# Mixer steps of a hybrid encoder block laid anew, and two of their products moved to GpSimd

## The chip, the cores and the metric

The kernel runs on one core of a Trainium2 chip. The metric is the device time of one launch in microseconds. Times of an unchanged kernel come as the median of several runs. The profile is that of one further execution. Engines are named as in the profile: PE is TensorE, DVE is VectorE, ACT is ScalarE, POOL is GpSimd, SP is SyncE.

## The reference

One block of a streaming encoder for 256 frames of width 2048, in float32. The input is normed, and one projection gives the columns of two mixers, which run side by side: a Mamba-2 mixer (four groups of eight heads) and an RWKV-7 mixer (32 heads of width 64). Their outputs go through one output projection, and a gated feed-forward layer of width 5632 and a last norm follow. The part that the change touches is the RWKV mixer:

```python
    kk = (k * k_k.astype(f32)).reshape(b, s, H, N)
    kk = kk / jnp.maximum(jnp.sqrt(jnp.sum(kk * kk, axis=-1, keepdims=True)), 1e-12)
    k = k * (1.0 + (a - 1.0) * k_a.astype(f32))
...
        sa = jnp.einsum('bhvk,bhk->bhv', S, a_t)
        S = S * w_t[:, :, None, :] + sa[..., None] * b_t[:, :, None, :] + v_t[..., None] * k_t[:, :, None, :]
        return S, jnp.einsum('bhvk,bhk->bhv', S, r_t)
```

The reference steps frame by frame. The result of each head is normed over its 64 columns, and to it is added a bonus, the sum of r k r_k over the head times the values v; then it is gated.

## The kernel before

Every big product is made as three passes of TensorE in a reduced float format: high part by high part, low by high and high by low. For that each weight tile, after its load (issued by SP in order), is cast on ACT to its high part whi (L192), and DVE subtracts it to get the low part wlo (L193). The raw tile, whi and wlo have four buffers each, so the two engines can be at most four tiles ahead of PE. `gemm_a` (L267) makes 96 matmuls of 128x256 in a call, 24 for each weight tile; `gemm_b` (L284) makes matmuls 512 wide, 12 for each tile.

The RWKV heads go in eight pairs of head groups, four heads to a pair, and the pair loop (L908) makes for each pair the projections k, v and r with `gemm_a`, and from pair 4 on, behind v, a quarter of an output projection with `gemm_b`. The small mixer work is cut into steps, closures that `rwkv_pair` (L444) makes: `keys2` (L520, with the key scale product kt at L526), `sums` (L548: products on DVE, the head sums `ps_sum` on PE, and the norms nn and bon), `amat` (L590, the score matrices atb and atk), `inv_out` (L628), `inv_level` and `inv_in` (L693), which send a small triangular matrix to memory and back and invert it there in blocks until X stands (L701), `lev16a` to `lev32b` (products `ps_b`), then for each of four chunks of 64 frames `step_r`, `step_w` and `step_s` (L755 to L823, matmuls `ps_r`, `ps_w`, `ps_s`, `ps_y`), and `gnorm`, `gnorm2` (the bonus product at L847) and `final`.

Where a step is issued is set by a queue: class `Side` (L42) holds steps with a due time in ticks, and the big product calls `side.tick` as it goes, four ticks for each call of `gemm_a`, so one tick is 24 matmuls. The tables PREP, AMATS, INV and CHAIN (L34 to L39) hold the due times. `window(pi, ticks)` (L882) fills the queue at the head of each pass of the loop: window pi runs the preparation of pair pi, the scores and inverse of pair pi-1 and the chain of pair pi-2. Windows 0 to 3 have 12 ticks, 4 to 7 have 16, window 8 has 20 and window 9 has 18. In windows of 12 ticks, the times of INV and CHAIN are scaled by 11.5/16. What is left at the end of a window is issued by `drain`. The framework then sets the final order on each engine by when operands are ready by its own costs.

Of the kernel before, what the change touches and what calls it, by code (L numbers as in the profile page):

```python
# [68 lines left out]
def tile_hybrid_block(ctx: ExitStack, tc: tile.TileContext, x, norm1_g, w_in, conv_w, conv_b, dt_bias, A_log, D_skip,  # L69
# [374 lines left out]
    def rwkv_pair(pi, st):  # L444
# [75 lines left out]
        def keys2():  # L520
            q, kp, ta, pin = (st[n] for n in ("q", "kp", "ta", "pin"))
            nc.vector.scalar_tensor_tensor(ta, ta, 1.0, q, ALU.add, ALU.mult)
            bt = tl("bt")
# [2 lines left out]
            nc.vector.tensor_tensor(kt, kp, pin, ALU.mult)  # L526
# [261 lines left out]
        def step_s(c):  # L788
# [34 lines left out]
            return f  # L823

        def gnorm():
            Y = st["Y"]
# [5 lines left out]
            for c in range(NCH):  # L832
                nc.scalar.activation(sq[:, c], Y[:, c], AF.Square, bias=nm[:, c:c + 1], accum_out=rs[:, c:c + 1])
            nc.scalar.activation(rs, rs, AF.Sqrt, bias=epsg, scale=1.0 / 64)
            nc.vector.reciprocal(rs, rs)
            nc.vector.tensor_tensor(nm, nm, rs, ALU.mult)
            for c in range(NCH):
                nc.scalar.activation(Y[:, c], Y[:, c], AF.Identity, bias=nm[:, c:c + 1], scale=rs[:, c:c + 1])

        def gnorm2():  # L840
            Y = st["Y"]
# [5 lines left out]
            nc.vector.tensor_tensor(vb, st["vt"], bc(st["bon"], 64), ALU.mult)  # L847
# [351 lines left out]
```

## Time and profile before

| what | value |
|---|---|
| median of three runs | 1671.96 us (1670.29, 1671.96, 1674.27) |
| the profiled execution's own time | 1671.13 us |
| its span, first to last instruction | 1669.4 us |
| mean granted TensorE clock | 0.996 |
| weights and inputs read from memory | 281.75 MB |

In the trace, window 0 begins at 38.1 us, window 1 at 76.6, window 2 at 117.8, window 3 at 185.9, window 4 at 242.2, window 5 at 309.0, window 6 at 376.5, window 7 at 443.7, window 8 at 510.6 and window 9 at 585.8 and ends at 652.9. The rest of the span is the Mamba mixer, the output projection and the feed-forward layer. A row of the table of windows has the stretch, its length, the busy time of each engine with its number of instructions, the granted clock and the DMA engines' share. A row of the timeline has the start, the duration, engine, line, operation, tiles out and in, and, in brackets, how long the engine stood idle and who released it.

### The profile page before, as it was taken

The numbers are of one execution on the slowest core, as the hardware profiler recorded it, in microseconds if no ns is written. First come the engines' busy times: TensorE is split into PE (matmuls) and PEld (weight loads), VectorE is DVE, ScalarE is ACT, GpSimd is POOL, SyncE is SP. The second block draws the span as 40 slices with busy tenths as digits, with TensorE's granted clock in tenths as the row PEclk, the third lists the DMA queues.
The fourth block names the chain that finished last, engine by engine and source line by source line (L and its number), as shares of the span: only waits on it lengthen the run. The fifth ranks groups of instructions, "written<-read, shape, count | busy, mean of one in ns | idle before, by whom it ended". The sixth has DMA issues, their size and how long they took to land.

```text
span 1669.4 us, 31147 instructions
## 1 busy us (share of the span) xinstructions
PE 1640.1 (98%) x12514; PEld 1422.7 (85%) x12514; DVE 1172.9 (70%) x1827; ACT 910.7 (55%) x1488; POOL 17.9 (1%) x57
## 2 busy tenths in 40 slices
PE   8999999999999999999999999999999999999997
PEld 8998898988888988998988888888888888888886
DVE  7887898788887867877778656465565564554657
ACT  6654775766755648657665544444444444444444
POOL 3000000000000000000000000000000000000000
PEclk9998999999999999999999999999999999999999
DMA  8653554454455556765655666666666666666663
GB/s 247 184 143 104 134 135 126 137 140 139 138 142 144 154 152 188 233 191 155 180 176 152 202 189 190 194 189 189 196 190 189 190 189 196 189 191 192 190 189 126
DMA packets 219473, 286.97 MB, mean 172 GB/s; under 512 B 41762, under 2 KB 124480, under 8 KB 218688
## 3 DMA queue, kind: packets, MB, share of 16 engines
q1 hardware_dynamic: 218000, 282.68, 58.1%
q8 instruction: 98, 1.61, 0.4%
q0 software_dynamic: 752, 1.24, 0.3%
q10 hardware_dynamic: 576, 1.05, 0.2%
q14 instruction: 47, 0.39, 0.1%
HBM read 281.75 MB, written 3.18 MB: 171 GB/s over the span
## 4 chain that ended last, share of the span: by engine, by line
PE 77%; DVE 9%; ACT 6%; issue 3%; DMA 3%; SPq 1%; DVEq 0%; POOL 0%; ACTq 0%
PE ps_o L305 8%; PE ps_o L306 8%; PE ps_o L307 8%; PE ps_gt L306 5%; PE ps_up L307 5%; PE ps_gt L305 5%; PE ps_up L306 5%; PE ps_gt L307 5%; PE ps_up L305 5%; DVE wlo L193 2%; PE ps_xs L277 2%; ACT whi L192 2%; PE ps_rkv L277 2%; PE ps_xs L278 2%; PE ps_xs L279 2%
## 5 line engine op out<-in xcount | busy, mean ns | idle before, releaser
L193 DVE TENSOR_TENSOR wlo<-raw,whi 128x1024 fp32r<-128x1024 f32 x508 | 619.9, 1222 | 376.9 <-ACT whi L192 375.8
L192 ACT CAST whi<-raw 128x1024 fp32r<-128x1024 f32 x508 | 532.7, 1051 | 596.8 <-PE ps_o L307 159.6
L277 PE MATMUL ps_rkv<-uh,whi 128*128 128x256 f32 x768 | 227.7, 296 | 0.0
L279 PE MATMUL ps_rkv<-uh,wlo 128*128 128x256 f32 x768 | 218.9, 285 | 0.0
L278 PE MATMUL ps_rkv<-ul,whi 128*128 128x256 f32 x768 | 218.8, 285 | 0.0
L277 PEld LDWEIGHTS ps_rkv<-uh,whi 128*128 128x128 f32 x768 | 147.5, 192 | 5.3 <-issue 0.7
L278 PEld LDWEIGHTS ps_rkv<-ul,whi 128*128 128x128 f32 x768 | 147.9, 193 | 1.2 <-issue 0.3
L279 PEld LDWEIGHTS ps_rkv<-uh,wlo 128*128 128x128 f32 x768 | 147.6, 192 | 0.4
L305 PE MATMUL ps_gt<-whi,uh 128*128 128x512 f32 x352 | 137.1, 389 | 0.0
L307 PE MATMUL ps_gt<-whi,ul 128*128 128x512 f32 x352 | 137.0, 389 | 0.0
L306 PE MATMUL ps_gt<-wlo,uh 128*128 128x512 f32 x352 | 136.9, 389 | 0.0
L305 PE MATMUL ps_up<-whi,uh 128*128 128x512 f32 x352 | 136.9, 389 | 0.0
L306 PE MATMUL ps_up<-wlo,uh 128*128 128x512 f32 x352 | 136.9, 389 | 0.0
L307 PE MATMUL ps_up<-whi,ul 128*128 128x512 f32 x352 | 136.9, 389 | 0.0
L305 PE MATMUL ps_o<-whi,ah 128*128 128x512 f32 x336 | 131.7, 392 | 0.0
L307 PE MATMUL ps_o<-whi,al 128*128 128x512 f32 x336 | 130.9, 390 | 0.0
L306 PE MATMUL ps_o<-wlo,ah 128*128 128x512 f32 x336 | 130.7, 389 | 0.0
L305 PE MATMUL ps_o<-whi,yh 128*128 128x512 f32 x256 | 105.6, 412 | 0.0
L307 PE MATMUL ps_o<-whi,yl 128*128 128x512 f32 x256 | 100.9, 394 | 0.0
L306 PE MATMUL ps_o<-wlo,yh 128*128 128x512 f32 x256 | 100.8, 394 | 0.0
L318 DVE TENSOR_TENSOR h<-ps_o,h 128x512 f32<-128x512 f32 x152 | 98.5, 682 | 1.7 <-PE ps_o L307 1.1
L306 PEld LDWEIGHTS ps_up<-wlo,uh 128*128 128x128 f32 x352 | 66.1, 188 | 13.7
(342 smaller groups left out, 2982.4 us busy)
## 6 DMA issues: line engine op xcount, KB each, us to landing
raw<-in_w_in_dram SPq DMA_DIRECT2D x180, 512.0 KB, 4.0
raw<-in_w_gate_dram SPq DMA_DIRECT2D x88, 512.0 KB, 3.7
raw<-in_w_up_dram SPq DMA_DIRECT2D x88, 512.0 KB, 3.7
raw<-in_w_down_dram SPq DMA_DIRECT2D x88, 512.0 KB, 4.6
raw<-in_w_out_dram SPq DMA_DIRECT2D x32, 512.0 KB, 4.0
raw<-in_w_out_dram SPq DMA_DIRECT2D x32, 256.0 KB, 4.2
raw<-in_w_out_dram SPq DMA_DIRECT2D x64, 128.0 KB, 4.0
csb<-cs_d SPq DMA_DIRECT2D x4, 1024.0 KB, 6.5
```

The costliest lines, as they stand in the source:

```text
L192: order(nc.scalar.copy(hi, raw))
L193: order(nc.vector.tensor_tensor(lo, raw, hi.bitcast(F32), ALU.subtract))
L277: nc.tensor.matmul(o, wh, uh[:, kt], start=first and b == 0, stop=False)
L278: nc.tensor.matmul(o, wh, ul[:, kt], start=False, stop=False)
L279: nc.tensor.matmul(o, wl, uh[:, kt], start=False, stop=last and b == 1)
L305: nc.tensor.matmul(ps[b], ah[:, s], hi[:, k], start=first, stop=False)
L306: nc.tensor.matmul(ps[b], ah[:, s], lo[:, k], start=False, stop=False)
L307: nc.tensor.matmul(ps[b], al[:, s], hi[:, k], start=False, stop=last)
L318: nc.vector.tensor_tensor(d, ps[b], d, ALU.add)
```

## The change

Five things are done. The step tables get new numbers, AMATS with eight entries for seven, CHAIN with twenty for sixteen. For windows of 12 ticks there are tables of their own, INV12 and CHAIN12, in place of the scaling. `sums` is cut in two, and the new step `norms` holds the head sums' matmuls and what is made of them. `gnorm` is cut in three (`gnorm`, `gscale`, `gapply`), and the bonus product becomes a step `bonus` of its own, in place over the values vt, with `cross_bonus` for the copies to the other half of the partitions. And GpSimd makes two products that DVE made: kt, and the bonus. Both are 128x512 in float32, one each for a pair, 16 in all. DVE has 16 products fewer; PE's matmuls are the same in number.

```diff
-AMATS = (0.132, 1.4, 2.027, 2.231, 2.69, 3.323, 6.493)
-INV = (4.9, 5.9, 6.9, 8.4, 10.4, 11.4, 12.9, 14.9)
+AMATS = (0.132, 1.6, 2.9, 3.1, 3.6, 3.9, 4.6, 6.6)
+INV = (5.9, 6.4, 8.1, 9.4, 11.4, 12.4, 13.4, 15.4)
+INV12 = (5.4, 5.9, 6.4, 7.4, 9.4, 10.4, 10.9, 11.9)
...
-            nc.vector.tensor_tensor(kt, kp, pin, ALU.mult)
+            nc.gpsimd.tensor_tensor(kt, kp, pin, ALU.mult)
...
             headsum(red[:, 1], rk)
+
+        def norms():
+            red = st["red"]
             ps = mxt("ps_sum")
...
+        def bonus():
+            vb = st["vt"]
+            nc.gpsimd.tensor_tensor(vb, vb, bc(st["bon"], 64), ALU.mult)
+
+        def cross_bonus():
+            st["vx"] = tl("vx", (P, 4, 64), 1, tag="t1")
+            for hh in range(2):
+                nc.scalar.copy(hd(st["vx"], 1 - hh), hd(st["vt"], hh)[:, 4:8])
...
-            vb = tl("ysq", (P, NCH, 64))
-            nc.vector.tensor_tensor(vb, st["vt"], bc(st["bon"], 64), ALU.mult)
-            vx = tl("vx", (P, 4, 64), 1, tag="t1")
-            for hh in range(2):
-                nc.scalar.copy(hd(vx, 1 - hh), hd(vb, hh)[:, 4:8])
+            vb, vx = st["vt"], st["vx"]
...
-        chain += [gnorm, gnorm2, final]
+        chain += [bonus, gnorm, gscale, gapply, cross_bonus, gnorm2, final]
...
-            for t, f in zip(INV, w["inv"]):
-                side.at(t if ticks >= 16 else t * (ticks - 0.5) / 16, f)
+            for t, f in zip(INV if ticks >= 16 else INV12, w["inv"]):
+                side.at(t, f)
...
-                side.at(t if ticks >= 16 else t * (ticks - 0.5) / 16, f)
+            for t, f in zip(CHAIN if ticks >= 16 else CHAIN12, pairs[pi - 2]["chain"]):
+                side.at(t, f)
```

The order of instructions moves on every engine. Three places follow. A row has the line, the operation, the tiles out and in, the shape and the number of equal instructions in a row; in the changed kernel the line numbers are two to sixteen higher.

The first is PE in window 2, where the first inverse reaches PE: `ps_b` from X is the first half of lev16a, `ps_b` from XT and t1s the second. Before:

```order
L712 MATMUL ps_b<-X,atb 32x32 x32
L279 MATMUL ps_rkv<-uh,wlo 128x256
L277 MATMUL ps_rkv<-uh,whi 128x256
L278 MATMUL ps_rkv<-ul,whi 128x256
...
L278 MATMUL ps_rkv<-ul,whi 128x256
L712 MATMUL ps_b<-XT,t1s 32x32 x32
```

Changed:

```order
L717 MATMUL ps_b<-X,atb 32x32 x32
L281 MATMUL ps_rkv<-uh,wlo 128x256
L279 MATMUL ps_rkv<-uh,whi 128x256
L280 MATMUL ps_rkv<-ul,whi 128x256
...
L279 MATMUL ps_rkv<-uh,whi 128x256
L717 MATMUL ps_b<-XT,t1s 32x32 x32
```

Six big matmuls stood between the two halves and eight stand there now. Ahead of the first half stand 635 big matmuls of `ps_rkv` in place of 620. On DVE, X stands behind 36 weight subtractions as before, and the last reduction ahead of X behind 34 in place of 33.

The second is window 3, about big matmuls 96 to 122 of the window. On PE, before, the head sums, the last two steps of one chunk and the first scores stood together, with single steps further on:

```order
L278 MATMUL ps_rkv<-ul,whi 128x256
L557 MATMUL ps_sum<-red,sel 128x16 x2
L796 MATMUL ps_s<-vt,ktt 64x64 x2
L799 MATMUL ps_s<-ws,btt 64x64 x2
...
L814 MATMUL ps_y<-vt,atk 64x64 x4
L814 MATMUL ps_y<-ws,atb 64x64 x4
L602 MATMUL ps_a<-ar,bt 64x128 x8
L619 MATMUL ps_a<-ar,bt 64x64 x8
L279 MATMUL ps_rkv<-uh,wlo 128x256
```

Changed:

```order
L281 MATMUL ps_rkv<-uh,wlo 128x256
L562 MATMUL ps_sum<-red,sel 128x16 x2
L607 MATMUL ps_a<-ar,bt 64x128 x8
L771 MATMUL ps_r<-vt,atk 64x64 x4
L771 MATMUL ps_r<-sn,ar 64x64 x4
L624 MATMUL ps_a<-ar,bt 64x64 x16
L785 MATMUL ps_w<-rs,XF 64x64 x4
L607 MATMUL ps_a<-ar,kt 64x128 x8
L801 MATMUL ps_s<-vt,ktt 64x64 x2
L279 MATMUL ps_rkv<-uh,whi 128x256
```

Now all scores and the r, w and s steps of a chunk stand behind the head sums without a big matmul between them. On DVE at the same place, before, weight subtractions (wlo) came at every third to eighth row:

```order
L193 TENSOR_TENSOR wlo<-raw,whi 128x1024
L538 STREAM_TRANSPOSE tmp_2801<-tmp 128x512
L539 TENSOR_REDUCE red<-tmp_2801 128x16
L490 SCALAR_TENSOR_TENSOR th<-smask,th 128x512
L560 TENSOR_SCALAR nn<-ps_sum 128x8
L565 COPY bon<-ps_sum 128x8
L561 RECIPROCAL nn<-nn 128x8
L807 TENSOR_TENSOR sn<-ps_s,pt 128x128
L193 TENSOR_TENSOR wlo<-raw,whi 128x1024
```

Changed; the first row is the subtraction for the tile of big matmul 96, and the next one, for the tile of 120, stands 37 rows behind it:

```order
L195 TENSOR_TENSOR wlo<-raw,whi 128x1024
L852 RECIPROCAL mv<-mv 128x8
L853 TENSOR_TENSOR mv<-mv 128x8
...
L541 TENSOR_REDUCE red<-tmp_2812 128x16
L884 TENSOR_TENSOR yl<-yc,yh 128x512
L500 COPY pt<-pr 128x8
L565 TENSOR_SCALAR nn<-ps_sum 128x8
...
L809 TENSOR_TENSOR sn<-ps_s,sn 128x128
```

Between the two subtractions there are now 36 other instructions of DVE: the end of one pair's chain, the head sums, the scores and a chunk's steps.

The third is PE in window 5, one of the windows with 16 ticks. Before:

```order
L279 MATMUL ps_rkv<-uh,wlo 128x256
L557 MATMUL ps_sum<-red,sel 128x16 x2
L780 MATMUL ps_w<-rs,XF 64x64 x4
...
L602 MATMUL ps_a<-ar,bt 64x128 x8
L619 MATMUL ps_a<-ar,bt 64x64 x16
L796 MATMUL ps_s<-vt,ktt 64x64 x2
L799 MATMUL ps_s<-ws,btt 64x64 x2
...
L814 MATMUL ps_y<-vt,atk 64x64 x4
L814 MATMUL ps_y<-ws,atb 64x64 x4
L277 MATMUL ps_rkv<-uh,whi 128x256
```

Changed:

```order
L804 MATMUL ps_s<-ws,btt 64x64 x2
L819 MATMUL ps_y<-vt,atk 64x64 x4
L819 MATMUL ps_y<-ws,atb 64x64 x4
L279 MATMUL ps_rkv<-uh,whi 128x256
...
L281 MATMUL ps_rkv<-uh,wlo 128x256
L562 MATMUL ps_sum<-red,sel 128x16 x2
L279 MATMUL ps_rkv<-uh,whi 128x256
...
L281 MATMUL ps_rkv<-uh,wlo 128x256
L607 MATMUL ps_a<-ar,bt 64x128 x8
L771 MATMUL ps_r<-vt,atk 64x64 x4
```

The chunk's s and y steps have moved ahead of the head sums, 12 big matmuls away; the head sums stand alone; and the first scores follow 12 big matmuls behind them, with the next chunk's r. The w step that stood with the head sums has moved too. There are 20 such bursts of small matmuls in the window, where there were 18.

More of the change, by code (lines that the diff above doesn't have):

```diff
@@ L34 @@
 PREP = (1.081, 1.2, 4.2, 5.2, 5.536, 6.756, 8.05, 9.2)
-AMATS = (0.132, 1.4, 2.027, 2.231, 2.69, 3.323, 6.493)
-INV = (4.9, 5.9, 6.9, 8.4, 10.4, 11.4, 12.9, 14.9)
+AMATS = (0.132, 1.6, 2.9, 3.1, 3.6, 3.9, 4.6, 6.6)
+INV = (5.9, 6.4, 8.1, 9.4, 11.4, 12.4, 13.4, 15.4)
+INV12 = (5.4, 5.9, 6.4, 7.4, 9.4, 10.4, 10.9, 11.9)
 STEPS = (0.667, 2.0, 5.0)
 SSD = (0.9, 2.7, 4.842, 6.642, 8.442, 8.924, 10.724, 12.524, 12.657, 16.124)
-CHAIN = (0.05, 0.6, 1.4, 2.4, 3.4, 4.0, 4.9, 5.9, 6.5, 7.4, 8.4, 9.0, 9.9, 11.4, 12.9, 13.4)
+CHAIN = (0.05, 0.4, 1.4, 2.4, 3.4, 4.4, 5.1, 6.1, 6.9, 7.6, 8.9, 9.9, 10.4, 10.45, 11.4, 12.4, 12.9, 13.1, 13.4, 13.9)
+CHAIN12 = (0.05, 0.4, 1.4, 2.4, 3.4, 4.4, 4.9, 5.9, 6.9, 7.4, 8.4, 9.4, 9.9, 9.95, 10.4, 10.9, 11.1, 11.2, 11.4, 11.9)
 class Side:
@@ L823, in step_s @@
             return f
+        def bonus():
[5 more added lines that the diff above has]
+                nc.scalar.copy(hd(st["vx"], 1 - hh), hd(st["vt"], hh)[:, 4:8])
         def gnorm():
             Y = st["Y"]
-            mv = tl("mv", (P, 2, NCH), 2)
+            st["mv"] = mv = tl("mv", (P, 2, NCH), 2)
             nm, rs = mv[:, 0], mv[:, 1]
@@ L833, in gnorm, with gscale @@
                 nc.scalar.activation(sq[:, c], Y[:, c], AF.Square, bias=nm[:, c:c + 1], accum_out=rs[:, c:c + 1])
+        def gscale():
+            nm, rs = st["mv"][:, 0], st["mv"][:, 1]
             nc.scalar.activation(rs, rs, AF.Sqrt, bias=epsg, scale=1.0 / 64)
@@ L836, in gnorm, with gapply @@
             nc.vector.tensor_tensor(nm, nm, rs, ALU.mult)
+        def gapply():
+            Y, nm, rs = st["Y"], st["mv"][:, 0], st["mv"][:, 1]
             for c in range(NCH):
@@ L868, in final @@
             nc.vector.tensor_tensor(yl, yo, yh.bitcast(F32), ALU.subtract)
-        amats = [recept, sums, amat("atb", "bt", 0), amat("atb", "bt", 1), inv_out, amat("atk", "kt", 0),
+        amats = [recept, sums, norms, amat("atb", "bt", 0), amat("atb", "bt", 1), inv_out, amat("atk", "kt", 0),
                  amat("atk", "kt", 1)]
@@ L891, in window @@
                 side.at(t, f)
-            for t, f in zip(INV, w["inv"]):
-                side.at(t if ticks >= 16 else t * (ticks - 0.5) / 16, f)
+            for t, f in zip(INV if ticks >= 16 else INV12, w["inv"]):
+                side.at(t, f)
         if pi > 1:
-            for t, f in zip(CHAIN, pairs[pi - 2]["chain"]):
-                side.at(t if ticks >= 16 else t * (ticks - 0.5) / 16, f)
+            for t, f in zip(CHAIN if ticks >= 16 else CHAIN12, pairs[pi - 2]["chain"]):
+                side.at(t, f)
     held = []
```

## The prediction

> **What bounds the kernel now.** I read the page's busy shares first, then the table of windows (one for each stretch of the pair loop), then TensorE's waits, then the timeline where those waits stand.
>
> ```profile
> PE 1640.1 (98%) x12514; PEld 1422.7 (85%) x12514; DVE 1172.9 (70%) x1827; ACT 910.7 (55%) x1488; POOL 17.9 (1%) x57
> ```
>
> TensorE is busy for 98% of a span of 1669.4 us, VectorE for 70%, GpSimd for 1%. The change touches no matmul of the big products, so all it can win is the 2% in which TensorE stands still, and the time in which it runs at a lower clock. The eight stretches in which mixer steps of the chain run are, in the table of windows:
>
> ```profile
> core 0: us, PE busy (x) PEld busy (x) DVE busy (x) ACT busy (x) POOL busy (x), PEclk, DMA share, GB/s
> 117.80:185.90 68.10, 62.69 (x998) 57.26 (x997) 53.95 (x109) 39.59 (x98) 1.00 (x5) 0.92 0.47 122
> 185.90:242.20 56.30, 54.87 (x805) 50.50 (x805) 50.91 (x103) 41.25 (x101) 0.56 (x3) 1.00 0.50 130
> 242.20:309.00 66.80, 65.48 (x855) 58.68 (x854) 57.37 (x111) 45.53 (x104) 0.55 (x3) 1.00 0.49 133
> 309.00:376.50 67.50, 65.57 (x854) 58.67 (x853) 57.47 (x111) 45.03 (x103) 0.56 (x3) 1.00 0.51 139
> 376.50:443.70 67.20, 65.49 (x855) 58.66 (x854) 57.56 (x111) 45.01 (x103) 0.56 (x3) 1.00 0.51 139
> 443.70:510.60 66.90, 65.45 (x855) 58.64 (x854) 57.62 (x111) 44.97 (x103) 0.56 (x3) 1.00 0.49 137
> 510.60:585.80 75.20, 74.47 (x943) 68.68 (x942) 62.18 (x117) 38.91 (x86) 0.00 (x0) 1.00 0.55 157
> 585.80:652.90 67.10, 66.83 (x570) 56.74 (x569) 46.26 (x85) 42.30 (x82) 0.00 (x0) 1.00 0.53 154
> ```
>
> These are windows 2 to 9. Length less PE busy gives TensorE's idle time in each: 5.41, 1.43, 1.32, 1.93, 1.71, 1.45, 0.73 and 0.27 us, 14.25 us in all. That is the ceiling of what shorter waits can give, apart from the clock. Window 2 alone holds 5.41 us, and its granted clock is 0.92. The waits by releaser:
>
> ```profile
> PE ps_b L712 <- DVE X L701: 2.9, 2, 2.2
> PE ps_r L766 <- DVE sn L805: 2.2, 5, 0.7
> PE ps_w L780 <- ACT rs L770: 2.0, 3, 0.8
> PE ps_y L814 <- DVE atb L622: 1.9, 4, 0.5
> PE ps_sum L557 <- DVE red L539: 1.6, 4, 0.5
> PE ps_b L712 <- ACT t1s L739: 1.3, 5, 0.6
> ```
>
> All are mixer steps whose operand came late: 11.9 us together. The timeline of window 6 shows a common one:
>
> ```profile
> 384.59 0.28 PE L278 MATMUL ps_rkv<-ul,whi 128*128 128x256 f32 x1
> 384.71 0.28 PE L279 MATMUL ps_rkv<-uh,wlo 128*128 128x256 f32 x1
> 385.45 0.59 PE L557 MATMUL ps_sum<-red,sel 128*128 128x16 f32 x4 [0.46 <-DVE red L539]
> 386.25 0.39 PE L277 MATMUL ps_rkv<-uh,whi 128*128 128x256 f32 x1
> 386.47 0.28 PE L278 MATMUL ps_rkv<-ul,whi 128*128 128x256 f32 x1
> 386.59 0.27 PE L279 MATMUL ps_rkv<-uh,wlo 128*128 128x256 f32 x1
> 390.18 0.28 PE L814 MATMUL ps_y<-vt,atk 64*64 64x64 f32 x3 [0.47 <-DVE atb L622]
> ```
>
> Starts of big matmuls stand 0.12 us apart (384.59, 384.71). The head sums wait 0.46 us for red, and the first big matmul behind the burst takes 0.22 us to the next instead of 0.12. With as much at its entry, I put 0.2 us on each additional burst.
>
> **The change part by part.** First, the steady windows 5, 6 and 7. In the new order the head sums stand alone, as the front part's rows of window 5 show: the products that VectorE reduces are issued at tick 1.6 and the sum's matmuls at 2.9, 1.3 ticks of 24 matmuls, 31 x 0.12 = 3.7 us later. The 0.46 us wait goes. The y step stood right behind the score matmuls and waited 0.47 us for VectorE's reads of their results; now it stands ahead of them, and that wait goes too. What is late next is r on sn and w on rs: r of the next chunk now follows the s and y steps after 24 or more matmuls, 2.9 us, where the longest wait of that kind was 0.7 us. I leave 0.3 us of idle time in each window of the 1.9, 1.7 and 1.45, thus minus 1.6, 1.4 and 1.15. Against that stand two more bursts in each window (20 for 18, counted in TensorE's order), 2 x 0.2 = 0.4 us. Net: about minus 1.2, 1.0, 0.8: **minus 3.0**. Windows 8 and 9 have 1.0 us of idle time between them. The same waits stand there, and I take all of it, the optimistic end: **minus 1.0**.
>
> Second, window 2. There lies the longest wait of the kernel:
>
> ```profile
> 122.95 0.28 PE L278 MATMUL ps_rkv<-ul,whi 128*128 128x256 f32 x1
> 125.47 1.73 PE L712 MATMUL ps_b<-X,atb 32*32 32x32 f32 x64 [2.25 <-DVE X L701]
> 131.23 0.41 PE L278 MATMUL ps_rkv<-ul,whi 128*128 128x256 f32 x1
> 131.45 0.41 PE L279 MATMUL ps_rkv<-uh,wlo 128*128 128x256 f32 x1
> 117.04 0.68 DVE L687 TENSOR_REDUCE xb<-pd 64x64 f32<-64x512 f32 x1
> 124.90 0.42 DVE L701 TENSOR_TENSOR X<-cm,pmask 128x256 f32<-128x256 f32 x1 [0.81 <-DMA cm<-sc_X]
> 117.80:150.30 32.50, 28.61 (x479) 0.84 0.49 127
> 128.60:134.50 5.90, 5.29 (x82) 0.50 0.35 93
> ```
>
> The last reduction of the small inverses ends at 117.7, its way through memory and back ends with X at 124.9, 7.2 us later, and TensorE has stood for 2.25 us. Behind it the granted clock is 0.50 (last row) and big matmuls come 0.213 us apart. In the new order 15 more big matmuls stand ahead of this step: 15 x 0.12 = 1.8 us, of which I count 1.6, since the reduction stands behind 34 weight subtractions and no longer 33. What is left of the wait is about 0.6 us, and rows with waits of that size show no drop of the clock. Some 22 big matmuls between 127 and 134.5 then start 0.093 us earlier each, 2.0 us. Of the 3.2 us of other idle time in this window I count a third, 1.0. Sum: **minus 4.6**. If the wait only moves, because the reduction comes later by one whole subtraction and its neighbours, this term is zero; if all idle time there went, it would be minus 7.4.
>
> The Trainium skill, "TensorE: Matmul & The Clock Gate", Part 1, has the clock halved after an idle window of about 3.4 us that runs on by itself. The trace agrees on the half (0.50) and shows it behind a wait of 2.25 us and 64 small matmuls. By a full window a wait under 3.4 us would not always cost it, and the 2.0 us would be chance.
>
> Third, windows 3 and 4. In the 12-tick windows the new order puts seven steps in one place: sums, scores, r, w and s stand between two big matmuls (the second pair of rows in the front part). TensorE's cost is not the burst but what VectorE has to do for it, beside the subtraction that it owes each weight tile:
>
> ```profile
> L193 DVE TENSOR_TENSOR wlo<-raw,whi 128x1024 fp32r<-128x1024 f32 x508 | 619.9, 1222 | 376.9 <-ACT whi L192 375.8
> ```
>
> Between the subtraction for the weight tile that starts at big matmul 96 of window 3 and the one for the tile at 120, there are now 36 other VectorE instructions; before, there was one subtraction for every three to eight rows. By the row of window 3, 50.91 us over 103 instructions, one takes 0.494 us, so 36 take 17.8. Four buffers let VectorE be four tiles ahead: matmuls 24 to 120 are 96 x 0.12 = 11.5 us, and the mixer matmuls in that stretch, which window 2 has handed on, add some 4 us. 17.8 less 15.5 is 2.3; the subtraction itself adds some of its 1.2 us. I take **plus 2.5** for window 3. In window 4, where the tail of window 3's inverse lies too, the same reckoning gives nearly 3 us, less 0.7 us of waits that go: **plus 2.3**. From below: if VectorE runs the small steps ahead while TensorE is still at matmuls before 24, both are zero. From above: 17.8 less 11.5 is 6.3 us each.
>
> Fourth, the two products. Their rows, and the nearest ones for GpSimd:
>
> ```profile
> L526 DVE TENSOR_TENSOR kt<-kp,pin 128x512 f32<-128x512 f32 x8 | 5.4, 678 | 0.0
> L847 DVE TENSOR_TENSOR ysq<-vt,bon 128x512 f32<-128x512 f32 x8 | 5.5, 686 | 5.3 <-ACT ysq L833 5.3
> L638 POOL MEMSET xb<- 64x272 f32 x8 | 2.6, 320 | 253.5 <-DMA sc_X<-xb 218.6 <-DVE ws L784 34.9
> L148 POOL TENSOR_SCALAR_AFFINE_SELECT trimask<-trimask 128x128 f32<-128x128 f32 x1 | 0.9, 919 | 0.0
> ```
>
> VectorE loses 5.4 + 5.5 = 10.9 us of 1172.9, 1.36 us in each window. VectorE stands idle 9 to 10 us in each 67 us window already (67.20 less 57.56), so by itself that is worth nothing; it helps the waits above, and I have counted them there. On GpSimd no product of 128x512 is in the trace. The fill does 272 columns in 0.32 us, hence 512 in 0.60; the select does 128 in 0.919, hence 512 in 3.7. I take 1.5 us, about the geometric middle, as the product reads two tensors and the fill none. Who waits: the key product may start when the previous pair's score matmuls have read kt, and VectorE transposes kt some 3 to 5 us later, so even 3.7 us is mostly hidden; if that cover went, VectorE would stand with the next weight subtractions behind it, and they are up to four tiles, 11.5 us, ahead. The bonus product waits for the last y step at matmul 222 and is needed at about 290, 8 us later. I put this part at **zero**, between minus 1 and plus 3.
>
> The Trainium skill, "SBUF — State Buffer", section "SBUF: two separate sides", says that a VectorE instruction with two inputs in SBUF and a GpSimd instruction that reads SBUF shut each other out for the whole instruction. That speaks against this change, and no row here shows it. By the Trainium skill, "GPSIMD Engine Reference", section 3.1, such a product of 2048 columns takes 4497 ns, by which an estimate for 512 is 1.1 us.
>
> The steps split off from gnorm (scale, apply, cross copies) run on ScalarE in the same number as before; ScalarE is at 55%, and I put them at zero.
>
> The sum: 1671.13 (the profiled execution; span 1669.4, median of the runs 1671.96, 0.83 above) minus 3.0 minus 1.0 minus 4.6 plus 2.5 plus 2.3 = 1671.13 minus 3.8 = **1667.3**. Two tenths of a per cent of the median, 3.3 us, is about what a measurement can tell here: faster means below 1668.6, slower above 1675.3.
>
> **The rivals.** *The crowded windows keep their cover.* VectorE reaches the crowded place early, so windows 3 and 4 lose nothing: 1667.3 less 4.8 = 1662.5; with the rest of the 14.25 us of idle time mostly gone too, 1657. For it: VectorE has 5.4 us idle in window 3 before the change. Against it: the 17.8 us without a subtraction are in the order itself. Chance 0.17.
>
> *GpSimd shuts VectorE out, or more bursts cost what waits gave.* If each product blocked VectorE for 1.5 us, that is 3.0 us in a window against 1.36 us saved, and operands come late by up to 1.6 us at two places; the 3.0 us of windows 5 to 7 are lost again: 1670.3. For it: the weight subtraction reads two tensors in SBUF and is over half of VectorE's busy time (619.9 of 1172.9 us). Against it: 10 us of spare time in each window. The Trainium skill's rule of the shared ports, cited above, would make it so. Chance 0.22, four fifths of it within 0.2%.
>
> *The crowded places stop TensorE long enough to lower the clock.* The point is a stop of about 2.25 us in one piece, as at 125.47: then some 22 matmuls of 0.213 us follow, 2.0 us, and with stops nearer the upper bound (3 us longer) each of windows 3 and 4 pays 5 us more: 1667.3 + 10 = 1677.3. For it: my own price for these stops, 2.3 and 3, lies at that point. Against it: the stop could come as several small ones, one for each late tile. Chance 0.20, and this is the slower side.
>
> **How the numbers follow.** The forecast, 1664 to 1670.5, has 0.41; it is the likeliest, so 1667.3 is the predicted time. Faster: 0.17 and 0.31 of the forecast's 0.41, 0.48. Same: 0.10 of the forecast and 0.18 of the second rival, 0.28. Slower: 0.20 of the third and 0.04 of the second, 0.24. The range takes in the first rival down to 1657 and the third up to 1679, one lowered clock above its price. The forecast's own range is 1664 to 1670.5.
>
> **What would show it.** Right: windows 5 to 7 each about 66.2 us, without rows of ps_sum waiting for red and of ps_y waiting for atb; X's wait in window 2 under 0.8 us and the clock 1.00 behind it; stops of two to three microseconds for wlo in windows 3 and 4, one row or two each; GpSimd products of 1 to 2 us. Wrong: no stop for wlo in windows 3 and 4, a second stretch with a clock of 0.5, VectorE's subtractions longer than 1.24 us where a GpSimd product runs, or windows 5 to 7 as long as before.

## The result, and the profile after

The changed kernel took 1684.68 us, the median of four runs (1682.89 to 1687.03), and the kernel before 1672.28 (1670.29 to 1674.27). The ratio is 1.0074, 95% interval 1.006 to 1.0088: slower by 0.7%, and outside the predicted range. One execution of run 13 below took 2729.29 us at a granted clock of 0.60; the median counts it, the ratio does not. The profiled execution took 1684.05 us, its span is 1682.3, and 1669.4 was the span before: 12.9 us to be found.

The page's busy shares after:

```profile
PE 1647.0 (98%) x12514; PEld 1425.5 (85%) x12514; DVE 1172.4 (70%) x1811; ACT 911.0 (54%) x1488; POOL 45.2 (3%) x73
```

VectorE has 16 instructions fewer, and is busy for as long as before: 1172.4 us for 1172.9. The 10.9 us that the two products took there have come back in other rows. TensorE is busy for 6.9 us more (1647.0 for 1640.1) with as many matmuls, and idle for 6.0 us more. The table of windows 2 to 9 after:

```profile
119.10:177.00 57.90, 53.78 (x766) 49.67 (x765) 44.85 (x84) 27.30 (x57) 2.14 (x6) 0.97 0.45 119
177.00:240.10 63.10, 59.61 (x806) 53.79 (x805) 48.84 (x100) 40.59 (x98) 2.52 (x4) 0.95 0.41 108
240.10:321.20 81.10, 74.99 (x1087) 65.38 (x1086) 66.45 (x132) 55.62 (x141) 4.69 (x8) 1.00 0.47 132
321.20:388.10 66.90, 65.79 (x855) 58.69 (x854) 57.09 (x107) 46.22 (x107) 5.10 (x5) 1.00 0.46 125
388.10:455.00 66.90, 65.76 (x854) 58.58 (x853) 58.46 (x108) 45.01 (x103) 5.10 (x5) 1.00 0.49 140
455.00:522.90 67.90, 65.86 (x855) 58.70 (x854) 58.72 (x109) 45.47 (x104) 4.29 (x5) 1.00 0.48 135
522.90:597.80 74.90, 74.90 (x943) 68.33 (x942) 62.88 (x116) 39.62 (x86) 1.76 (x1) 1.00 0.57 164
597.80:664.00 66.20, 66.20 (x571) 56.86 (x570) 43.99 (x71) 41.51 (x81) 1.04 (x1) 1.00 0.54 160
```

Windows 2, 3 and 4 have to be read together, since their matmuls have moved between them: 766, 806 and 1087 for 998, 805 and 855, 2659 and 2658 in all. They took 202.1 us after and 191.2 before: plus 10.9. By the rows TensorE is busy there for 188.4 us after and 183.0 before, and idle for 13.7 and 8.2: about half of the loss is waiting, and half is a longer busy time for the same matmuls. Windows 5 to 7 took 201.7 and 201.6: no change. Windows 8 and 9 took 141.1 and 142.3: minus 1.2. Window 0 begins 1.8 us later, windows 0 and 1 give back 0.5 us, and the part behind window 9 is 1.9 us longer. That makes the 12.9.

The longer busy time does not come from the clock. The stretches at half the clock add up to 10.2 us in windows 2 to 4 both before (first row) and after (second and third); the fourth row, after too, lies in window 4 and is needed further on:

```profile
125.50:135.70 10.20, 9.59 (x184) 8.81 (x184) 6.38 (x11) 1.07 (x2) 0.12 (x1) 0.50 0.45 128
130.50:133.90 3.40, 3.40 (x76) 3.11 (x76) 2.51 (x5) 0.20 (x1) 0.00 (x0) 0.50 0.30 51
181.70:188.50 6.80, 6.80 (x113) 5.93 (x114) 5.19 (x14) 2.04 (x6) 1.04 (x1) 0.50 0.30 80
248.10:252.60 4.50, 4.50 (x117) 3.89 (x115) 3.12 (x9) 2.03 (x5) 1.04 (x1) 1.00 0.38 120
```

Big matmuls that follow one another in these windows start 104.9 us apart in sum before and 104.8 after. So the time lies in and beside the bursts of small matmuls, which stand in another order; why they take longer is open.

TensorE's waits after:

```profile
PE ps_b L717 <- DVE X L706: 7.5, 5, 2.5
PE ps_y L819 <- DVE ws L789: 2.9, 4, 0.8
PE ps_yc L1056 <- DVE y L1053: 1.7, 1, 1.7
PE ps_y L819 <- DVE atk L610: 1.6, 1, 1.6
```

The waits of the head sums for red and of y for atb, which stood in this list before, are gone. X has grown from 2.9 us in two waits to 7.5 in five. The timeline shows the three long ones, at the head of windows 2, 3 and 4, and in window 2 the last reduction and X:

```profile
120.60 0.70 DVE L692 TENSOR_REDUCE xb<-pd 64x64 f32<-64x512 f32 x1
128.27 0.43 DVE L706 TENSOR_TENSOR X<-cm,pmask 128x256 f32<-128x256 f32 x1 [1.67 <-DMA cm<-sc_X]
128.84 1.11 PE L717 MATMUL ps_b<-X,atb 32*32 32x32 f32 x64 [2.51 <-DVE X L706]
180.58 1.11 PE L717 MATMUL ps_b<-X,atb 32*32 32x32 f32 x64 [2.21 <-DVE X L706]
247.02 1.11 PE L717 MATMUL ps_b<-X,atb 32*32 32x32 f32 x64 [2.08 <-DVE X L706]
```

Before, windows 3 and 4 had no such wait at their heads: the inverse was done by the end of windows 2 and 3. Now it is handed on to the next window, where TensorE reaches it before it is back from memory. Behind the wait in window 2 the clock is down for 3.4 us, behind that in window 3 for 6.8, and behind that in window 4, of 2.08 us, not at all (the fourth of the rows above).

GpSimd's two products, by the groups of instructions:

```profile
L832 POOL TENSOR_TENSOR vt<-vt,bon 128x512 f32<-128x512 f32 x8 | 15.4, 1924 | 161.1 <-PE ps_y L819 161.1
L528 POOL TENSOR_TENSOR kt<-kp,pin 128x512 f32<-128x512 f32 x8 | 12.1, 1511 | 212.7 <-PE ps_w L785 137.6 <-PE ps_a L607 27.0 <-ACT whi L194 26.1
```

The means are 1.51 us for the key product and 1.92 for the bonus; the shortest rows are 1.28 and 1.04. What they do to VectorE is in the timelines of windows 5 and 6:

```profile
352.51 1.28 POOL L528 TENSOR_TENSOR kt<-kp,pin 128x512 f32<-128x512 f32 x1 [22.18 <-PE ps_w L785]
352.86 2.01 DVE L195 TENSOR_TENSOR wlo<-raw,whi 128x1024 fp32r<-128x1024 f32 x1
433.06 3.31 POOL L832 TENSOR_TENSOR vt<-vt,bon 128x512 f32<-128x512 f32 x1
433.11 2.35 DVE L195 TENSOR_TENSOR wlo<-raw,whi 128x1024 fp32r<-128x1024 f32 x2
369.47 0.41 ACT L837 COPY vx<-vt 64x256 f32<-64x256 f32 x1 [2.45 <-POOL vt L832]
```

A weight subtraction that begins while the key product runs ends after 2.01 us in place of 1.22. It is done 1.08 us after the product's end, about as if it had begun only then. At 433 it is the other way: two subtractions take their usual 2.35 us together, and the product, which stands beside them, lasts 3.31 us in place of 1.04. In the whole trace 11 VectorE instructions beside GpSimd's products are longer than their like by 0.17 to 1.00 us, 6.7 us in all. The last row is a wait of ScalarE for the bonus, one of seven.

### The profile page after: what moved, and what is told of

Its sections match the earlier page's. It is cut to its first block, busy times and chain, and to the rows that moved or that the text cites. A ratio compares the mean times of both kernels' runs of the same rounds, so it can differ in the third digit from the quotient of the medians.

```text
span 1682.3 us, 31128 instructions
## 1 busy us (share of the span) xinstructions
PE 1647.0 (98%) x12514; PEld 1425.5 (85%) x12514; DVE 1172.4 (70%) x1811; ACT 911.0 (54%) x1488; POOL 45.2 (3%) x73
## 3 DMA queue, kind: packets, MB, share of 16 engines
q0 software_dynamic: 752, 1.24, 0.3%
## 4 chain that ended last, share of the span: by engine, by line
PE 80%; DVE 8%; ACT 5%; DMA 5%; issue 2%; SPq 1%; POOL 0%; DVEq 0%; ACTq 0%; POOLq 0%
PE ps_o L307 7%; PE ps_o L309 7%; PE ps_o L308 7%; PE ps_gt L308 5%; PE ps_gt L307 5%; PE ps_up L309 5%; PE ps_up L308 5%; PE ps_up L307 5%; PE ps_gt L309 5%; PE ps_rkv L279 4%; PE ps_rkv L281 3%; PE ps_rkv L280 3%; DVE wlo L195 2%; PE ps_xs L279 2%; PE ps_xs L280 2%
## 5 line engine op out<-in xcount | busy, mean ns | idle before, releaser
L308 PEld LDWEIGHTS ps_up<-wlo,uh 128*128 128x128 f32 x352 | 66.1, 188 | 13.7
```

Of the source, the lines that this page charges most:

```text
L308: nc.tensor.matmul(ps[b], ah[:, s], lo[:, k], start=False, stop=False)
```

## The experiments

Two theories stood at the start. T: the due times for the windows of 12 ticks are what costs. G: GpSimd and VectorE shut each other out. Each ratio is to the kernel before as it was timed beside that run (medians 1671.76 to 1672.42 us). The windows are those of one profiled execution, whose time stands in the fourth column and can lie 5 us off the median; the idle time is their length less TensorE's busy time:

| run | median us | ratio to before, 95% interval | profiled, us | windows 2 to 4 | idle in 2 to 4 | windows 5 to 7 |
|---|---|---|---|---|---|---|
| before | 1672.28 | | 1671.13 | 191.2 | 8.2 | 201.6 |
| changed | 1684.68 | 1.0074 (1.006 to 1.0088) | 1684.05 | 202.1 | 13.7 | 201.7 |
| 1: changed, products on VectorE | 1675.01 | 1.0011 (0.9997 to 1.0025) | 1673.44 | 196.6 | 8.6 | 198.6 |
| 2: before, products on GpSimd | 1692.73 | 1.0124 (1.0104 to 1.0144) | 1695.27 | 196.9 | 14.1 | 212.7 |
| 3: changed, old 12-tick times | 1674.09 | 1.0014 (1.0001 to 1.0028) | 1673.81 | 192.2 | 10.0 | 203.0 |
| 4: as 3, products on VectorE | 1670.76 | 0.9989 (0.9969 to 1.0008) | 1671.46 | 193.5 | 10.2 | 198.5 |
| 5: as 1, idle products on GpSimd | 1680.77 | 1.0054 (1.0036 to 1.0071) | 1685.53 | 201.0 | 11.8 | 204.5 |
| 6: as 1, idle fills on GpSimd | 1677.10 | 1.0027 (1.0007 to 1.0046) | 1673.31 | 195.2 | 9.7 | 200.1 |
| 7: as 3, kt alone on GpSimd | 1669.63 | 0.9981 (0.9967 to 0.9995) | 1669.56 | 190.4 | 9.4 | 200.5 |
| 8: as 3, the bonus alone on GpSimd | 1677.76 | 1.0034 (1.0022 to 1.0046) | 1674.60 | 196.2 | 12.0 | 199.6 |
| 9: changed, about the old 12-tick times of the inverse | 1687.78 | 1.0101 (1.0085 to 1.0116) | 1690.35 | 206.4 | 15.3 | 205.2 |
| 10: changed, old 12-tick times of scores and chain | 1678.99 | 1.0051 (1.0035 to 1.0066) | 1674.53 | 194.3 | 12.3 | 201.7 |
| 11: as 7, more time for X's way | 1670.52 | 0.9984 (0.997 to 0.9998) | 1672.56 | 191.0 | 9.9 | 203.3 |
| 12: changed, old 12-tick times of the scores | 1683.30 | 1.0058 (1.0038 to 1.0078) | 1686.47 | 201.2 | 14.0 | 203.5 |
| 13: changed, old 12-tick times of the chain | 1675.92 | 1.0016 (0.9999 to 1.0032) | 1677.90 | 194.9 | 10.0 | 203.5 |

**Run 1, both products back on VectorE.**

```diff
-            nc.gpsimd.tensor_tensor(kt, kp, pin, ALU.mult)
+            nc.vector.tensor_tensor(kt, kp, pin, ALU.mult)
...
-            nc.gpsimd.tensor_tensor(vb, vb, bc(st["bon"], 64), ALU.mult)
+            nc.vector.tensor_tensor(vb, vb, bc(st["bon"], 64), ALU.mult)
```

> The changed kernel with both products back on VectorE; tables and split steps stay. Theory T (the tables for the 12-tick windows cost it: windows 2, 3 and 4 took 57.9 + 63.1 + 81.1 = 202.1 us after, 191.2 before): windows 2 to 4 still take over 198 us and the time stays at 1677 to 1683. Theory G (GpSimd and VectorE shut each other out, and the late VectorE costs it): back to 1670 to 1673, and windows 2 to 4 under 193 us. Both expect the long VectorE rows (a weight subtraction of 2007 ns at 352.86 us) to be gone.

The time fell by 9.7 us, windows 2 to 4 by 5.5, windows 5 to 7 by 3.1:

```profile
118.80:180.50 61.70, 57.55 (x958) 53.40 (x957) 50.38 (x98) 28.93 (x67) 0.92 (x5) 0.97 0.46 123
180.50:233.70 53.20, 52.24 (x613) 47.62 (x613) 44.92 (x90) 38.14 (x88) 0.12 (x1) 1.00 0.43 116
233.70:315.30 81.60, 78.08 (x1086) 67.81 (x1086) 66.41 (x134) 57.64 (x144) 0.99 (x5) 0.96 0.44 120
315.30:381.30 66.00, 65.58 (x855) 58.65 (x854) 57.71 (x110) 44.98 (x105) 0.56 (x3) 1.00 0.52 142
381.30:447.30 66.00, 65.58 (x854) 58.62 (x854) 58.40 (x111) 44.73 (x103) 0.56 (x3) 1.00 0.53 142
447.30:514.00 66.70, 65.63 (x855) 58.66 (x853) 58.40 (x111) 44.95 (x103) 0.56 (x3) 1.00 0.50 138
```

Neither theory alone holds. By itself the new order gives 3.0 us in windows 5 to 7 (198.6 for 201.6), with 0.4 us of idle time in windows 5 and 6, and GpSimd takes them back. Windows 2 to 4 stay 5.4 us above before without GpSimd, and that is not waiting: by these rows TensorE is idle there for 8.6 us, as before (8.2), and busy for 187.9, nearly as after the change (188.4). The page of this run says the same of the whole:

```profile
PE 1647.1 (99%) x12514; PEld 1426.7 (85%) x12514; DVE 1174.5 (70%) x1827; ACT 909.5 (54%) x1488; POOL 18.2 (1%) x57
```

TensorE's 7.0 us of additional busy time are there without GpSimd's products, so they belong to the new order. The order in windows 2 to 4 is not quite that of the change: the framework places some steps differently when it reckons with another engine, and one inverse is no longer handed over the end of window 2. How much of the waiting that is missing here is due to GpSimd alone can't be read from this pair; run 5 says more.

**Run 2, the kernel before with only the two products on GpSimd.** The bonus stays in `gnorm2`, right ahead of the additions that use it.

```diff
-            nc.vector.tensor_tensor(kt, kp, pin, ALU.mult)
+            nc.gpsimd.tensor_tensor(kt, kp, pin, ALU.mult)
...
-            nc.vector.tensor_tensor(vb, st["vt"], bc(st["bon"], 64), ALU.mult)
+            nc.gpsimd.tensor_tensor(vb, st["vt"], bc(st["bon"], 64), ALU.mult)
```

> The kernel before with only the two products on GpSimd; tables and steps as before. Theory T: within 2 us of the kernel before, windows 2 to 4 at 190 to 193 us. Theory G: slower by 8 to 13 us. The 16 products would lengthen VectorE instructions by 0.5 to 1.0 us each in either.

It lost over 20 us, more than either theory said. Windows 5 to 7 took 3.3 to 4.0 us more each, with a granted clock below 1:

```profile
316.20:387.00 70.80, 66.98 (x855) 60.14 (x854) 58.01 (x110) 45.43 (x105) 4.33 (x5) 0.98 0.46 126
387.00:458.20 71.20, 68.16 (x854) 61.31 (x853) 57.56 (x109) 44.86 (x103) 3.54 (x5) 0.95 0.48 132
458.20:529.00 70.80, 67.23 (x855) 60.11 (x854) 57.56 (x109) 45.04 (x103) 4.19 (x5) 0.98 0.45 129
```

In the whole kernel TensorE waits for red, the products of the head sums, for 7.6 us in four waits, where it was 1.6 in four before:

```profile
PE ps_sum L557 <- DVE red L539: 7.6, 4, 3.4
```

Two of these waits, 3.8 us together, stand in windows 5 to 7, with one of 2.4 us for kp in window 5; the longest, 3.4 us, stands in window 8. So the old order suffers from GpSimd more than the new one. That the split steps are what spares the new order is argued; no run has the split alone.

**Run 3, the old times in the 12-tick windows.** The steps stay as they are cut, with `norms` right behind `sums` and `bonus` right behind the last s step.

```diff
+AMATS12 = (0.132, 1.4, 1.4, 2.027, 2.231, 2.69, 3.323, 6.493)
...
-INV12 = (5.4, 5.9, 6.4, 7.4, 9.4, 10.4, 10.9, 11.9)
+INV12 = (3.522, 4.241, 4.959, 6.038, 7.475, 8.194, 9.272, 10.709)
...
-CHAIN12 = (0.05, 0.4, 1.4, 2.4, 3.4, 4.4, 4.9, 5.9, 6.9, 7.4, 8.4, 9.4, 9.9, 9.95, 10.4, 10.9, 11.1, 11.2, 11.4, 11.9)
+CHAIN12 = (0.036, 0.431, 1.006, 1.725, 2.444, 2.875, 3.522, 4.241, 4.672, 5.319, 6.038, 6.469, 7.116, 7.152, 8.194, 8.194, 8.194, 9.272, 9.272, 9.631)
```

The line of AMATS stays for the other windows; `window` takes AMATS12 in windows of 12 ticks.

> The changed kernel with the times of before (AMATS, and INV and CHAIN scaled by 11.5/16) in the windows of 12 ticks, for the steps as they are cut now; the windows of 16 ticks and more keep the new tables, and GpSimd keeps its products. Theory T: windows 2 to 4 back to 190 to 193 us and the time at 1670 to 1674. Theory G: no change from 1684.7 by more than 4 us.

As T said, to 0.1 us: windows 2 to 4 fell by 9.9 us, the time by 10.6.

**Run 4, run 3 with both products on VectorE.** To run 3's edit comes that of run 1:

```diff
-            nc.gpsimd.tensor_tensor(kt, kp, pin, ALU.mult)
+            nc.vector.tensor_tensor(kt, kp, pin, ALU.mult)
...
-            nc.gpsimd.tensor_tensor(vb, vb, bc(st["bon"], 64), ALU.mult)
+            nc.vector.tensor_tensor(vb, vb, bc(st["bon"], 64), ALU.mult)
```

> As the run with the old times in the 12-tick windows, and both products back on VectorE: the new order in the windows of 16 ticks by itself. Theory T: 1669 to 1672, windows 5 to 7 at 66.2 to 66.9 us, without the wait of the s step at big matmul 192 (0.45 and 0.94 us after). Theory G: about 1672, as the kernel before.

Windows 5 to 7 took 66.0, 66.0 and 66.6 us. The ratio's interval holds 1, so it can't be told from the kernel before.

**Runs 5 and 6, GpSimd working for nobody.** Both add to run 1 work on GpSimd whose result nothing reads; the products that count are VectorE's. TensorE's and VectorE's order is row by row that of run 1. Run 5:

```diff
             nc.vector.tensor_tensor(kt, kp, pin, ALU.mult)
+            nc.gpsimd.tensor_tensor(ta, kp, pin, ALU.mult)
...
+            jk = tl("ysq", (P, NCH, 64))
+            nc.gpsimd.tensor_tensor(jk, vb, bc(st["bon"], 64), ALU.mult)
             nc.vector.tensor_tensor(vb, vb, bc(st["bon"], 64), ALU.mult)
```

Run 6 against run 5:

```diff
-            nc.gpsimd.tensor_tensor(ta, kp, pin, ALU.mult)
+            nc.gpsimd.memset(ta, 0.0)
...
-            nc.gpsimd.tensor_tensor(jk, vb, bc(st["bon"], 64), ALU.mult)
+            nc.gpsimd.memset(jk, 0.0)
```

> The new tables with both products made by VectorE, as in the run at 1675.01 us, and beside them the same two products made by GpSimd once more into dead tiles, which nothing reads; TensorE's and VectorE's order is the same as in that run, row by row. Theory L (GpSimd's reads shut VectorE out while they last): the lengthened VectorE rows of 0.5 to 1.0 us are there, windows 5 to 7 go from 66.0 + 66.0 + 66.7 us to about 201.6 in sum as after the change, and the time to 1678 to 1682. Theory W (what costs is waiting for GpSimd's slower result, and the order laid for it): windows 5 to 7 stay within 0.5 us of 198.7, the time within 2 us of 1675.

> As the run with the idle products, but each is a fill of the same 128x512 tile, which reads nothing. Theory L: windows 5 to 7 at 198.7 us and the time at 1675, no VectorE row lengthened by over 0.2 us. Theory W: the same. A difference between this run and the one with the products is the price of GpSimd's reads alone.

In run 5 the same kind of row as after the change, in window 7:

```profile
457.32 1.04 POOL L834 TENSOR_TENSOR ysq<-vt,bon 128x512 f32<-128x512 f32 x1 [24.12 <-DVE yl L887]
457.77 1.68 DVE L195 TENSOR_TENSOR wlo<-raw,whi 128x1024 fp32r<-128x1024 f32 x1
```

In run 6 a fill in window 3 that meets a subtraction at its start:

```profile
211.35 0.53 POOL L529 MEMSET ta<- 128x512 f32 x1 [11.34 <-DVE bt L526]
211.43 1.18 DVE L195 TENSOR_TENSOR wlo<-raw,whi 128x1024 fp32r<-128x1024 f32 x1
```

In run 5 ten VectorE rows beside the products are longer by 0.45 to 0.76 us, 5.7 us in all; in run 6 no row beside a fill of 0.53 us is, though two subtractions run beside one for 0.4 us or more. So it is the product that shuts VectorE out, not that GpSimd is at work. In run 5 TensorE is idle for 11.8 us in windows 2 to 4, for 8.6 in run 1 with the same order. Of the time the medians say 2.1 us from run 1 to run 6, 3.7 from there to run 5, and 3.9 more to the changed kernel, whose results are waited for and whose order differs. Neighbouring steps of this ladder overlap in their intervals; run 1 and run 5 don't. The windows of run 5 come from its slowest execution (1685.53 of 1678.05 to 1685.53) and overstate the difference.

**Runs 7 and 8, one product at a time on GpSimd,** with the rest as in run 4. Run 7 against run 4:

```diff
-            nc.vector.tensor_tensor(kt, kp, pin, ALU.mult)
+            nc.gpsimd.tensor_tensor(kt, kp, pin, ALU.mult)
```

Run 8 against run 4:

```diff
-            nc.vector.tensor_tensor(vb, vb, bc(st["bon"], 64), ALU.mult)
+            nc.gpsimd.tensor_tensor(vb, vb, bc(st["bon"], 64), ALU.mult)
```

> Old times in the 12-tick windows, new tables elsewhere, kt on GpSimd and the bonus on VectorE. With both on GpSimd it was 1674.09 us and windows 5 to 7 203.0, with both on VectorE 1670.76 and 198.6. Theory L: the key product, which falls on the weight subtractions and the inverse's products, brings most of it: 201 to 203 us in windows 5 to 7 and 1673 us. Theory W: kt has 3 to 5 us of cover, so under 0.5 us of change.

> As the run before it with the two products exchanged: the bonus on GpSimd, kt on VectorE. Theory L: the bonus starts while X is due and lengthens X's row (0.43 us without, 0.65 to 1.18 after the change), 199 to 200 us in windows 5 to 7 and 1671 to 1672. Theory W: 8 us of cover, no change from 198.6.

Theory L had the halves the wrong way round. The key product costs 2.0 us in windows 5 to 7, and the whole is the best version that was measured, 0.19% under the kernel before (interval 0.05 to 0.33%) though not told apart from run 4. The bonus alone costs 1.1 us in windows 5 to 7, and 7.0 us in the median. In its trace ScalarE waits for the bonus for 14.2 us in six waits, to copy it to the other half of the partitions, and TensorE for X for 10.7 us in seven waits; that either is the way of its cost is argued, not shown. The expectation for run 8, 1671 to 1672 us, was missed by 6.

**Runs 9, 10, 12 and 13, which of the 12-tick tables costs.** All start from the changed kernel with both products on GpSimd. Run 9, where the first two entries are still later than the old 3.522 and 4.241:

```diff
-INV12 = (5.4, 5.9, 6.4, 7.4, 9.4, 10.4, 10.9, 11.9)
+INV12 = (4.3, 4.5, 4.96, 6.04, 7.48, 8.2, 9.27, 10.7)
```

Run 10 has both lines that follow, run 12 the first alone, run 13 the second alone:

```diff
+AMATS12 = (0.132, 1.4, 1.4, 2.027, 2.231, 2.69, 3.323, 6.493)
...
+CHAIN12 = (0.036, 0.431, 1.006, 1.725, 2.444, 2.875, 3.522, 4.241, 4.672, 5.319, 6.038, 6.469, 7.116, 7.152, 8.194, 8.194, 8.194, 9.272, 9.272, 9.631)
```

> The changed kernel with the inverse's due times in the 12-tick windows earlier again, about those of before (4.3, 4.5, 4.96, 6.04, 7.48, 8.2, 9.27, 10.7); AMATS and CHAIN12 stay new, GpSimd keeps both products. Theory I (the inverse was laid so late that it spills past the window's end and TensorE stands for X at the head of windows 3 and 4): windows 2 to 4 go from 202.1 us to under 196 and the time to about 1677. Theory C (the chain's and the scores' steps are crowded into the end of the window, and the inverse spills because it comes behind them): 200 us or more, 1682 or more. In TensorE's order the inverse still spills into windows 3 and 4 here, which speaks for C.

> The changed kernel with the times of before for scores and chain in the 12-tick windows, and the new late times for the inverse (INV12); GpSimd keeps both products. Theory I: windows 2 to 4 stay near 202 us and the time above 1680. Theory C: under 195 us, 1674 to 1676, as with all the old times (192.2 us, 1674.09).

> The changed kernel with the scores' times of before (AMATS) in the 12-tick windows; CHAIN12 and INV12 stay new, GpSimd keeps both products. Theory S (the later head sums and scores crowd the windows and push the inverse over the end): windows 2 to 4 under 196 us in place of 202.1, the time about 1678. Theory K (the chain's table does it: its last w and y steps at 9.4 and 9.9 of 11.5 ticks are left to the window's end, where they stand behind the inverse): 199 us or more and over 1681, since in TensorE's order the last w and y of the chain still stand with the inverse at big matmul 234 of window 2 and 278 of window 3.

> The changed kernel with the chain's times of before in the 12-tick windows; AMATS and INV12 stay new, GpSimd keeps both products. Theory S: 199 us or more in windows 2 to 4, over 1681. Theory K: 194 to 196 us, as with scores and chain both of before (194.3 us, 1678.99), the time 1677 to 1680.

Windows 2 to 4 of run 12 and of run 13:

```profile
119.90:185.60 65.70, 59.63 (x998) 54.68 (x997) 49.81 (x98) 33.96 (x85) 3.83 (x7) 0.97 0.46 123
185.60:240.60 55.00, 50.57 (x655) 47.05 (x653) 47.52 (x93) 34.51 (x73) 2.57 (x4) 1.00 0.52 141
240.60:321.10 80.50, 77.02 (x1006) 66.89 (x1005) 64.52 (x127) 58.77 (x147) 4.70 (x6) 0.94 0.38 102
```

```profile
118.70:183.90 65.20, 60.25 (x935) 54.60 (x934) 51.69 (x105) 37.13 (x91) 4.17 (x7) 0.95 0.48 126
183.90:245.80 61.90, 58.71 (x871) 53.24 (x869) 51.19 (x104) 42.31 (x104) 3.54 (x5) 0.97 0.42 112
245.80:313.60 67.80, 65.97 (x857) 58.75 (x854) 58.51 (x109) 45.77 (x107) 5.10 (x5) 1.00 0.45 122
```

The chain's table alone brings 7.2 of the 10.9 us back; the scores' alone brings 0.9, and the inverse's alone loses another 4.3. So it wasn't the inverse's own due times that drove it over the window's end: in run 9, which has them earlier, it still spills. The intervals of run 13 and of the changed kernel stand apart; those of runs 9 and 12 touch it. CHAIN12 puts the last w and s steps at 9.4 and 9.9 of 12 ticks. In TensorE's order of the changed kernel they stand with the inverse at the end of the window or in the next one, and from window 3 on the work of one window is done in the next. The count of matmuls shows it: 1087 and 1006 in window 4 with the new chain, 857 with the old.

That the chain's table costs is shown; by which way is not. The inverse that is handed over is not the whole of it. In run 12 the first products from X stand inside windows 2 and 3 again, at big matmuls 242 and 286, and windows 2 to 4 take 201.2 us all the same, with 14.0 us of idle time in many smaller waits. In run 13 TensorE is idle for 10.0 us and busy for 184.9, so of the 7.2 us one half is waiting and one half busy time. Run 10 also speaks against a sum of single parts: with the old scores beside the old chain its median is 3.1 us above run 13's, not below, and over the 1674 to 1676 us that were expected; its windows come from its fastest execution.

**Run 11, more time for X's way through memory.** Against run 7:

```diff
-INV12 = (3.522, 4.241, 4.959, 6.038, 7.475, 8.194, 9.272, 10.709)
+INV12 = (3.3, 3.7, 4.2, 4.6, 8.6, 9.4, 10.4, 11.4)
```

> The best so far (old times in the 12-tick windows for scores and chain, new tables elsewhere, kt alone on GpSimd, 1669.63 us) with the inverse's steps in the 12-tick windows at 3.3, 3.7, 4.2, 4.6, 8.6, 9.4, 10.4, 11.4, so that the way through memory has 4.0 ticks until lev16a in place of 1.4. If X's way is what window 2 to 4 still lose by, X's waits there (2.45 us the longest in the like run with both products on VectorE) get shorter, and the time is 1666 to 1669; if the waits only move, 1669 to 1671.

It only moved the waits: 191.0 us in windows 2 to 4 for 190.4. But its window 7 took 70.0 us, 2.7 more than in run 7, with the same due times. The timeline and the table of windows there:

```profile
493.62 1.11 PE L718 MATMUL ps_b<-X,atb 32*32 32x32 f32 x64 [1.78 <-DVE mv L845]
494.66 0.69 PE L308 MATMUL ps_o<-whi,yh 128*128 128x512 f32 x1
495.15 0.63 PE L309 MATMUL ps_o<-wlo,yh 128*128 128x512 f32 x1
495.58 0.63 PE L310 MATMUL ps_o<-whi,yl 128*128 128x512 f32 x1
...
493.60:498.10 4.50, 4.48 (x74) 0.63 0.42 123
```

TensorE waited 1.78 us at the product from X (the row names mv, which VectorE made right behind X), and behind that its 512-wide matmuls start 0.43 us apart in place of 0.23, at a granted clock of 0.63. In run 7 at the same place:

```profile
491.68 1.11 PE L718 MATMUL ps_b<-X,atb 32*32 32x32 f32 x64 [0.61 <-DVE mv L845]
491.70:496.20 4.50, 4.50 (x136) 1.00 0.49 148
```

There the wait was 0.61 us, and the clock stayed at 1.00. The steps' due times in this window are the same; the wait came out 1.2 us longer, and with the slow matmuls behind it the window 2.7. The length of a wait alone does not decide on the clock: behind the 2.08 us in window 4 of the changed kernel it stayed at 1.00, as shown above.

## Why the prediction was wrong

The step that failed is the third, windows 3 and 4, and with it the second; the fourth, the two products at zero, failed too. The sum had minus 4.6 for window 2 and plus 2.5 and 2.3 for windows 3 and 4, 0.2 together; they came to plus 10.9. The third step says that TensorE's cost is not the burst but what VectorE has to do for it, lays the price on VectorE's row of 36 instructions without a weight subtraction, and looks for stops for wlo. There is no such stop in window 3 and there are two in window 4, of 0.96 and 0.72 us. The crowded burst of window 3 cost TensorE a wait of 0.31 us for pr and one of 0.61 us within it.

What the runs show in its place has two parts. One is 5.3 us of additional busy time of TensorE in windows 2 to 4 (188.4 for 183.0), for which the sum had no term beyond 0.2 us for each additional burst. Run 1 has nearly all of it without GpSimd's products (187.9), and run 13, with the old chain's table, has 184.9: the new 12-tick tables bring it, the chain's table most of it. Why the small matmuls take longer in that order stays open. The other part is 5.6 us more of waiting (13.7 for 8.2), of which the waits for X are 4.6 (7.5 for 2.9). That the inverse goes over the window's end could be read from the order (lev16a of window 3's pair stood in window 4), but it was taken for work that is merely done elsewhere, at no price. With the new tables and the products on VectorE the waiting is 8.6 us (run 1), and with the old tables and both products on GpSimd it is 10.0 (run 3), so in the changed kernel the two act together.

For window 2 the prediction gave X 1.6 us more cover. TensorE did come 15 matmuls later, but the last reduction ended at 121.3 us, 2.2 us after the start of the window, where before it had ended at 117.7, 0.1 us ahead of it. The wait was 2.51 us for 2.25. The text named this as its lower case, "if the wait only moves", at zero. The half clock lasted 3.4 us in window 2 and not 10.2, but window 3 had the other 6.8.

Windows 5 to 7 were predicted at minus 3.0 for the order, with GpSimd at zero. Run 1 measures the order at minus 3.0, and the waits that were to go are gone. That the number is the same is in part luck: idle time fell by 3.2 us and not by 4.2, and the six additional bursts cost 0.3 us of busy time and not 1.2. The failed term is GpSimd's: plus 3.1 there by run 1 against the changed kernel, and part of windows 2 to 4 as well. The products' durations (1.5 us estimated; means of 1.51 and 1.92) were near. The cover of kt held, since VectorE waited for it once, for 1.2 us, but it was beside the point: VectorE is stopped while kt is made. The cover of the bonus did not hold: ScalarE waits for it seven times, 22.0 us in all. That was the second rival's mechanism, at 0.22, and its price of 3.0 us for these windows fits; it had no price for the other windows. The Trainium skill, "SBUF — State Buffer", section "SBUF: two separate sides", gives the rule for a VectorE instruction with two inputs in SBUF and a GpSimd instruction that reads SBUF: whichever of the two starts first has the ports for the whole instruction. The trace agrees that either can hold up the other (2.01 for 1.22 us, and 3.31 for 1.04), and run 6 agrees that a GpSimd instruction that reads nothing does not stop VectorE. On who comes first it agrees in the first pair of rows alone: in the second the product's start is recorded 0.05 us ahead of the subtraction's, and it is still the product that stands.

Windows 8 and 9 were right: minus 1.2 for minus 1.0. The third rival, on the slower side, was right in its sign and its 1677.3 too small, and its mechanism, a stop at the crowded place, is not what happened. Its point from which the clock falls, a wait of about 2.25 us, is no fixed one: 1.78 us sufficed in run 11, and 2.08 us in window 4 did not. Three of the signs of being wrong that the prediction names came: subtractions longer than 1.24 us beside a product, a second stretch at half the clock (window 3), and windows 5 to 7 as long as before.

Two pieces stay open. Window 0 begins at 38.1 us before and at 38.8 to 40.6 in all other kernels' profiles, whose prologue is the same; whether the 1.8 us are a run's luck is not shown. The 1.9 us behind window 9 are for the larger part a wait of TensorE for y of 1.7 us (L1053, in the table of waits above); run 12 has it too, 1.9 us, run 13 with 1.2 and run 8 with 0.6, the other runs have not, and its cause is open.

## What to carry to other kernels

A new order of the same matmuls can make TensorE busy for longer, here by 7.0 us in 1640, so compare its busy time and not only its waits. A step that is handed over a window's end isn't sure to be free work elsewhere: ask what latency it waits on at the place where it now stands first, and how many matmuls are left there to cover it. An idle GpSimd isn't a free engine for VectorE's products: count the VectorE instructions that will meet each product; here a copy with one input was held up too (0.86 us for 0.17, beside the key product at 158.55 us). And test a change of an order's tables and a change of engine apart; here the one was worth minus 3 us in windows 5 to 7, and the other took it back.

## What the runs showed of the hardware

A 128x512 float32 product took on GpSimd 1.04 us (the bonus) and 1.28 us (the key product) at its shortest, and 0.68 us on VectorE; beside VectorE's subtractions it was stretched to as much as 3.31 us. A fill of the same tile took 0.53 us. The granted clock fell to one half for 3.4, 6.8 or 10.2 us at a time. It did so behind a wait of TensorE of 1.78 us (run 11), and not behind one of 2.08 us (window 4 of the changed kernel) or of 0.61 us (run 7).
